# Mixer A's heads in two passes, branch products in pieces beside them, and the out product made once

## The chip, the cores and the metric

The kernel runs on one core of one Trainium2 chip. The metric is the device time of one execution in microseconds (us). TensorE (PE) does the matmuls, VectorE (DVE), ScalarE (ACT) and GpSimd (POOL) work elementwise, and SyncE (SP) issues nearly all DMA transfers. Each engine runs its own instruction list strictly in the order in which it was written, and waits at semaphores for the others.

## The reference, cut to what matters

One layer of an encoder with two parallel mixers, over 1024 prompt tokens and 32 new tokens of another stream, which the kernel lays side by side as 1056 columns:

```python
h = rmsnorm(x) @ w_in          # -> q/k/v and indexer of mixer A, q/k/v of mixer B, gates ga, gb
o_a = sparse_attention(...)    # mixer A, 8 heads of 64: top-k mask, softmax
o_b = stick_breaking(...)      # mixer B, 8 heads of 64: sigmoid products from the right
m = sigmoid(ga) * (o_a @ w_branch_a) + sigmoid(gb) * (o_b @ w_branch_b)
h = x + m @ w_out              # 1024 x 1024
y = h + relu(rmsnorm(h) @ w_up)**2 @ w_down      # 1024 -> 4096 -> 1024
```

All of it is float32.

## The kernel before

**Three matmuls for one product.** Every float32 operand is split into a high part `h` (a cast to `fp32r` on ACT) and a low part `l = x - h` (on POOL or DVE). A product is three matmuls: `wh xh + wh xl + wl xh` (`three`). A weight unit is a 128x512 tile: its DMA to `wst`, its cast on ACT (`wh`) and its subtraction on POOL (`wl`); five such units can be held at a time (`WB`).

**Column blocks.** `column_block` makes one 128-row block of a product over all tokens, in the chunks `self.parts`: columns 0-511, 512-783 and 784-1055 (widths 512, 272, 272). Columns 0-511 are "tile 0" of a pair of tiles, columns 512-1055 "tile 1" (`pick`).

**Attention.** `attend(h, is_a)` makes one head. It has two halves: `i = 0` for query tiles t = 0 to 3 (128 tokens each) and `i = 1` for t = 4 to 7. For each query tile there are scores against all earlier keys (PE, tile `s`), for mixer A a masked maximum on DVE, an exponential on ACT, a reciprocal on DVE and a normalisation on POOL (tile `p`). For each pair of query tiles follow transposes (PE, `t<-ident,p`), a split of the transposed weights into two parts (ACT cast and DVE subtraction, tile `tt`), the product with the values (PE, `o<-tt,v`), and `halves`, which adds the two parts (ACT copy and DVE addition, tile `o`) before the output goes to DRAM (`do`). Keys, values and queries are loaded from DRAM for each head. `attend_new` does the 32 new tokens of four heads at once.

**Work beside the heads.** The gate products (16 blocks `gate(e)`, 8 of each mixer) and the branch products of mixer B (8 blocks `branch_b(e)`, all three chunks at once) are put between the heads by `GATES_BESIDE` and `BRANCH_BESIDE`. A `with nc.behind()` makes each DMA recorded in it wait for the last instruction recorded before it, that is for the store of the head before.

**The order.** The kernel records its operations in a list and places them itself (`Plan`): an operation runs when what it needs is there, by rank (`FAST`, `PREP`, `MAIN`, `FILL`), and the matmuls of column blocks have the rank `FILL`, behind those of attention. So the order on each engine is fixed when the program is built, by a table of assumed costs. All operations are recorded at one line of the kernel, L387, so the profile's rows are told apart by tile names.

**After the heads.** `merge` loads mixer A's head outputs (`load_o`, tile `oa`), makes the branch product of mixer A (tile `ft` takes gate times product, POOL adds mixer B's part `y`, and ACT and DVE split the sum into `mh` and `ml`), and then the out product: for tokens 0-511 all eight blocks `e` in chunks of 256, then for tokens 512-1055 all eight in chunks of 272, so that each of the 16 units of `w_out` is loaded and split twice. After each block from the fifth on, `h_forms` cuts the result (tile `y`) into high and low parts of sums and differences that the FFN needs as operands: seven forms, `B11`, `B21` in `xl`, `T1`, `B22` in `oa`, `T2`, `T3` in `mh` and `T4` in `ml`. Those in `mh` and `ml` overwrite the out product's own operands.

**The FFN** (`ffn`, `down`) takes the seven forms in the order B11, B21, T1, T2, T3, T4, B22, 24 matmuls of 256 or 272 columns each, per pair of row blocks.

Of the kernel before, what the change touches and what calls it, by code (L numbers as in the profile page):

```python
# [27 lines left out]
H = 8  # L28
# [16 lines left out]
GATES_BESIDE = (1, 1, 1, 1, 1, 1, 1, 0, 1, 0, 0, 0, 0, 0, 0, 0)  # L45
BRANCH_BESIDE = (0, 0, 0, 0, 2, 2, 2, 2)
# [348 lines left out]

class Layer:
# [82 lines left out]
    def run(self):  # L479
# [113 lines left out]
        todo = iter(range(KB))  # L593
        for h in range(H):
            self.attend(h, True)
            if h in (2, 5):
                self.attend_new(h // 3, True)
            with nc.behind():
                for _ in range(GATES_BESIDE[H + h]):
                    self.gate(next(gates), "gz", 3)  # L600
                if h == 3:
                    self.yy = [nc.tile(xp, [128, KB, n], F32, f"y{i}", tag=f"xh{i}") for i, n in enumerate((W1, T - W1))]
                    ob = self.xl
                    self.load_o(ob, 4, range(4))
                for _ in range(BRANCH_BESIDE[h]):
                    self.branch_b(next(todo), ob)
# [486 lines left out]
    def attend(self, h, is_a):  # L1093
# [33 lines left out]
        for i in range(2):  # L1127
# [28 lines left out]
    def attend_new(self, u, is_a):  # L1156
# [92 lines left out]
    def branch(self, name, e, o, done):  # L1249
# [3 lines left out]
            [unit], lambda k, cs: (self.pick(o, k, cs), self.pick(o, 4 + k, cs)), done, self.parts, kn=4)  # L1253

    def branch_b(self, e, o):

        nc = self.nc
        with nc.rank(PREP):
            nc.sync.dma_start(self.yy[0][:, e], self.dg[KB + e, :, 0:W1])
# [6 lines left out]
        self.branch("w_bb", e, o, done)  # L1266
# [15 lines left out]
    def merge(self):  # L1282

        nc, a, f32 = self.nc, self.a, lambda z: z.bitcast(F32)
        self.load_o(self.oa, 0, range(4))
        high = lambda k, cs: self.pick(self.mh, k, cs)
        low = lambda k, cs: self.pick([z[k // 4] for z in self.ml], k % 4, cs)
        sgs = self.ring(self.temps(self.ft, 4, 0, 544))
        for e in range(KB):

            def done(c, cs, ps, e=e):
# [5 lines left out]
                h, l = high(e, cs), low(e, cs)  # L1297
                nc.scalar.copy(h, sg)
                nc.vector.tensor_sub(l, sg, f32(h))

            self.branch("w_ba", e, self.oa, done)
# [10 lines left out]
        slots = self.ring(self.temps(self.ft, 9, 0, 272))  # L1312
        acc = self.rb
        for i in range(2):
            n, lo = QUADS[i]
            chunks = [slice(lo, lo + n), slice(lo + n, lo + 2 * n)]
            for e in (0, 4, 1, 5, 2, 6, 3, 7):
                units = [self.unit(a["w_out"][e, j]) for j in range(2)]

                def done(c, cs, ps, e=e, n=n):  # L1320
                    hs = slots()[:, :n]
                    with nc.rank(PREP):
                        nc.sync.dma_start(hs, a["xT"][:, e, cs])
                    nc.vector.tensor_add(hs, ps, hs)
                    nc.sync.dma_start(self.dh[e, :, cs], hs)
                    nc.scalar.activation(self.pick(self.yy, e, cs), hs, AF.Copy, scale=self.gf[:, e:e + 1])
                    if e == 0:
                        nc.scalar.activation(acc[:, cs], hs, AF.Square)
                    else:
# [16 lines left out]
    def cut(self, i, f, k, x):  # L1346
# [4 lines left out]
        nc.gpsimd.tensor_sub(l, x, h.bitcast(F32))  # L1351
# [336 lines left out]
```

## Time and profile before

| | |
|---|---|
| times of three runs | 1751.46, 1755.16, 2347.33 us; median 1755.16 us |
| profiled execution | 1752.31 us, span 1750.2 us |
| PE, PEld busy | 1705.4 us (97%), 1619.5 us (93%), 12584 matmuls |
| DVE, ACT, POOL busy | 1294.6 (74%), 948.7 (54%), 1000.7 us (57%) |
| HBM | 187.29 MB read, 86.78 MB written, 157 GB/s over the span |
| mean granted TensorE clock | 0.998 |

The span is the time from the first to the last instruction on the core. A matmul's shown duration overlaps the next one's: what one costs is the distance between two starts. Stages in the span: mixer B's heads from about 500 us, mixer A's from about 700 to 907 us, the branch product of A from 923 to 975 us, the out product to 1078 us, the FFN to the end.

### The profile page before, as it was taken

Reading aid. Unit: us, or ns where it says so; the run is one execution under the profiler, and the core shown is the slowest. Engines: PE = TensorE matmul, PEld = TensorE weight load, DVE = VectorE, ACT = ScalarE, POOL = GpSimd, SP = SyncE. Lnnn points to the kernel's source line nnn. Section 1 sums busy time; section 2 is a strip of 40 time slices with the busy share of each in tenths; the row PEclk is TensorE's granted clock in tenths of the full one; section 3 lists DMA queues with packets and bytes.
Section 4 is the critical chain, followed back from the end, with each engine's and each line's share of the span. In section 5 each row is a group of like instructions: output and inputs, shape, how many; then the busy total and the mean of one; then the engine's idle time right before and its main releaser. Section 6 shows DMA issues by size and latency. Waiting matters only on the chain. (4 is left out here: it accounts for less than half of the span.)

```text
span 1750.2 us, 35569 instructions
## 1 busy us (share of the span) xinstructions
PE 1705.4 (97%) x12584; PEld 1619.5 (93%) x12584; DVE 1294.6 (74%) x2678; ACT 948.7 (54%) x1997; POOL 1000.7 (57%) x863
## 2 busy tenths in 40 slices
PE   7999999999999999998899999999999999999998
PEld 7988898999989998897798998999999999999998
DVE  8577899999477988776654546876666696787667
ACT  7356888732367777898743565333333354335431
POOL 5822331344277676344638899876667775464442
PEclk9999999999999999999999999999999999999999
DMA  7233553444574555545654564344444486657644
GB/s 253 73 98 109 147 158 102 123 148 128 158 201 114 155 137 158 138 125 150 175 164 148 175 188 118 129 149 142 140 150 141 143 313 226 218 166 240 225 143 149
DMA packets 182338, 276.52 MB, mean 158 GB/s; under 512 B 30353, under 2 KB 71921, under 8 KB 182161
## 3 DMA queue, kind: packets, MB, share of 16 engines
q1 hardware_dynamic: 181728, 273.91, 51.0%
q8 instruction: 99, 1.62, 0.4%
q14 instruction: 79, 0.64, 0.1%
q10 hardware_dynamic: 432, 0.34, 0.1%
HBM read 187.29 MB, written 86.78 MB: 157 GB/s over the span
## 5 line engine op out<-in xcount | busy, mean ns | idle before, releaser
L387 POOL TENSOR_TENSOR wl<-wst,wh 128x512 fp32r<-128x512 f32 x197 | 274.0, 1400 | 222.4 <-ACT wh L387 204.9
L387 PE MATMUL pj<-xl,wh 128*128 128x272 f32 (+2 forms) x1232 | 349.9, 318 | 1.6 <-DVE ft L387 1.2
L387 PE MATMUL pj<-xh,wh 128*128 128x272 f32 (+1 forms) x768 | 251.6, 328 | 2.6 <-ACT wh L387 1.6
L387 PE MATMUL pj<-xh,wl 128*128 128x272 f32 (+1 forms) x768 | 252.0, 329 | 0.4 <-POOL wl L387 0.4
L387 PEld LDWEIGHTS pj<-xl,wh 128*128 128x128 f32 x1232 | 219.4, 188 | 15.5 <-DVE ft L387 1.5
L387 ACT CAST wh<-wst 128x512 fp32r<-128x512 f32 x197 | 120.9, 620 | 128.0 <-PE pj L387 25.1
L387 POOL TENSOR_TENSOR wl<-us,wh 128x512 fp32r<-128x512 f32 x80 | 119.7, 1502 | 115.9 <-ACT wh L387 114.3
L387 PEld LDWEIGHTS pj<-xh,wh 128*128 128x128 f32 x768 | 144.7, 188 | 13.5 <-ACT wh L387 1.8
L387 PEld LDWEIGHTS pj<-xh,wl 128*128 128x128 f32 x768 | 144.5, 188 | 11.5 <-POOL wl L387 0.6
L387 POOL TENSOR_TENSOR wl<-y,wh 128x512 fp32r<-128x512 f32 x79 | 109.2, 1387 | 39.6 <-ACT wh L387 37.9
L387 ACT CAST wh<-us 128x512 fp32r<-128x512 f32 x80 | 49.6, 621 | 142.6 <-DVE us L387 38.3
L387 DVE TENSOR_TENSOR_SCAN rem<-rem 128x384 f32<-128x384 f32 (+8 forms) x66 | 114.8, 1761 | 14.8 <-ACT rem L387 12.4
L387 POOL TENSOR_TENSOR p<-p,rem 128x383 f32<-128x383 f32 (+8 forms) x66 | 102.1, 1566 | 40.3 <-DVE rem L387 20.8
L387 DVE TENSOR_TENSOR tt<-t,tt 128x512 fp32r<-128x512 f32 (+2 forms) x168 | 99.7, 619 | 16.8 <-ACT tt L387 16.1
L387 PE MATMUL o<-tt,v 128*128 128x256 f32 (+1 forms) x640 | 100.4, 284 | 11.0 <-ACT tt L387 5.3
L387 PEld LDWEIGHTS o<-tt,v 128*128 128x128 f32 x640 | 90.9, 192 | 19.9 <-ACT tt L387 7.0
L387 PE MATMUL s<-k,q 128*128 128x512 f32 (+3 forms) x384 | 100.8, 358 | 3.3 <-DVE mx L387 1.3
L387 ACT ACTIVATE junk<-score,cand 128x1024 bf16<-128x1024 f32 (+2 forms) x93 | 96.9, 1042 | 12.3 <-DVE cand L387 11.0
L387 PE MATMUL s<-wh,xh 128*128 128x256 f32 (+1 forms) x360 | 101.0, 286 | 2.5 <-DVE small L387 1.9
L387 PE MATMUL s<-wh,xl 128*128 128x256 f32 (+1 forms) x360 | 100.9, 283 | 0.0
L387 PE MATMUL s<-wl,xh 128*128 128x256 f32 (+1 forms) x360 | 100.6, 282 | 0.0
L387 ACT CAST tt<-t 128x512 fp32r<-128x512 f32 (+2 forms) x168 | 84.9, 540 | 26.6 <-PE o L387 13.2
(326 smaller groups left out, 5592.6 us busy)
## 6 DMA issues: line engine op xcount, KB each, us to landing
us<-w_down SPq DMA_DIRECT2D x96, 256.0 KB, 2.9
q<-dq SPq DMA_DIRECT2D x64, 256.0 KB, 4.2
du<-y SPq DMA_DIRECT2D x56, 264.0 KB, 2.1
du<-us SPq DMA_DIRECT2D x56, 264.0 KB, 2.3
y<-w_up SPq DMA_DIRECT2D x44, 256.0 KB, 2.7
xl<-du SPq DMA_DIRECT2D x35, 264.0 KB, 5.4
mh<-du SPq DMA_DIRECT2D x35, 264.0 KB, 5.3
dv<-vs SPq DMA_DIRECT2D x32, 256.0 KB, 2.6
```

The source lines that it names most:

```text
L387: fn(*args, **kw)
```

## The change

- `attend` takes `passes`. Mixer A's heads run in two passes: first all eight heads with `passes=(0,)` (query tiles 0 to 3), then all eight with `(1,)` (query tiles 4 to 7, for which the first half of keys and values is loaded again).
- Five gate blocks instead of seven lie beside mixer B's heads, and three instead of one beside A's.
- The branch products are cut into pieces of one token part: `branch_b0(e)` (B, columns 0-511, gated, stored back to `dg` in DRAM), `branch_b1(e)` (B, the other two chunks, into `y`), `branch_a0(e)` (A, columns 0-511, added to `y` on POOL). A list of 27 pieces (3 gates, 8 + 8 + 8) is handed out beside the 16 half heads by `FILL_BESIDE`, each weight unit being loaded once per piece.
- `merge` makes only chunks 1 and 2 of A's branch product, and splits columns 0-511 of `y` that are there already.
- The out product runs once over all tokens: eight blocks `e` with chunks 512, 272, 272. The square of the result is put back into PSUM by ACT, and DVE, not POOL, adds it up. `h_forms` runs for both token parts after each block from the fifth on, and the cuts for T2 (subtraction now on DVE), T3 and T4 follow for both parts at the end.

```diff
-GATES_BESIDE = (1, 1, 1, 1, 1, 1, 1, 0, 1, 0, 0, 0, 0, 0, 0, 0)
-BRANCH_BESIDE = (0, 0, 0, 0, 2, 2, 2, 2)
+GATES_BESIDE = (1, 1, 1, 1, 1, 0, 0, 0)
+FILL_BESIDE = (1, 1, 1, 1, 2, 2, 2, 2, 2, 2, 2, 2, 2, 2, 2, 2)
...
+        fill = [(lambda e: self.gate(e, "gz", 3), e) for e in gates]
+        fill += [(self.branch_b0, e) for e in range(KB)]
+        fill += [(self.branch_b1, e) for e in range(KB)]
+        fill += [(self.branch_a0, e) for e in range(KB)]
+        fill = iter(fill)
...
         for h in range(H):
-            self.attend(h, True)
+            self.attend(h, True, (0,))
+            beside(FILL_BESIDE[h])
+        for h in range(H):
+            self.attend(h, True, (1,))
             if h in (2, 5):
                 self.attend_new(h // 3, True)
...
+            beside(FILL_BESIDE[H + h] if h < H - 1 else None)
+        self.load_o(self.xl, 0, range(1, 2))
...
+    def branch_a0(self, e):
...
+        y = self.yy[0][:, e]
+        with nc.rank(PREP):
+            nc.sync.dma_start(y, self.dg[KB + e, :, 0:W1])
+        self.gated("w_ba", e, self.dg[e], lambda z: nc.gpsimd.tensor_add(y, y, z))
...
-        for i in range(2):
-            n, lo = QUADS[i]
-            chunks = [slice(lo, lo + n), slice(lo + n, lo + 2 * n)]
-            for e in (0, 4, 1, 5, 2, 6, 3, 7):
...
+        for e in (0, 4, 1, 5, 2, 6, 3, 7):
+            units = [self.unit(a["w_out"][e, j]) for j in range(2)]
...
-                        sq = slots()[:, :n]
-                        nc.scalar.activation(sq, hs, AF.Square)
-                        nc.gpsimd.tensor_add(acc[:, cs], acc[:, cs], sq)
+                    nc.scalar.activation(ps, hs, AF.Square)
+                    nc.vector.tensor_add(acc[:, cs], ps, acc[:, cs])
...
+        for f, eng in ((T2, nc.vector), (T3, nc.gpsimd), (T4, nc.gpsimd)):
+            for i in range(2):
                 for k in range(4):
-                    self.cut(i, f, k, self.h_parts(i, k)[{T2: 3, T3: 0, T4: 2}[f]])
+                    self.cut(i, f, k, self.h_parts(i, k)[{T2: 3, T3: 0, T4: 2}[f]], eng)
```

**First place: PE where mixer A begins.** Rows of PE shortly after mixer B's last head (`s`, `t`, `o` are attention; `pj` is a gate block with its weights `wh`, `wl`). Before:

```order
L387 MATMUL pj<-xl_108,wh_6828 128x272
L387 MATMUL pj<-xh_107,wl_6829 128x272
L387 MATMUL pj<-xh_105,wh_6916 128x512
L387 MATMUL pj<-xl_106,wh_6916 128x512
L387 MATMUL pj<-xh_105,wl_6917 128x512
L387 MATMUL o<-tt,v 128x256
L387 MATMUL pj<-xh_105,wh_6916 128x512
L387 MATMUL pj<-xl_106,wh_6916 128x512
L387 MATMUL pj<-xh_105,wl_6917 128x512
L387 MATMUL pj<-xh_105,wh_6916 128x512
L387 MATMUL o<-tt,v 128x256 x4
```

After the change, behind the same two rows of the last gate block (`wh_6828`, `wl_6829`):

```order
L387 MATMUL pj<-xl_108,wh_6828 128x272
L387 MATMUL pj<-xh_107,wl_6829 128x272
L387 MATMUL o<-tt,v 128x256 x5
L387 MATMUL t<-ident,p 128x128 x3
L387 MATMUL o<-tt,v 128x256 x3
L387 MATMUL t<-ident,p 128x128 x4
L387 MATMUL s<-k,q 128x256 x2
L387 MATMUL s<-k,q 128x384 x2
L387 MATMUL o<-tt,v 128x256
L387 MATMUL s<-k,q 128x512 x2
L387 MATMUL s<-k,q 128x128 x2
L387 MATMUL o<-tt,v 128x256
```

The next gate block has moved back: behind these two rows come 42 rows of half heads without a `pj` matmul, and then the first of the three gates.

**Second place: POOL at the end of mixer A, after the change.** `wl..<-wst` is a weight unit's low part, `y0<-y0,gz` the addition of one `branch_a0` piece, `xl1` the low part of A's head outputs, `ft<-ft,y1` an addition in `merge`:

```order
L387 TENSOR_TENSOR y0_7311<-y0_7311,gz_7718 128x512
L387 TENSOR_TENSOR wl4_7774<-wst_7772,wh4_7773 128x512
L387 TENSOR_TENSOR y0_7311<-y0_7311,gz_7723 128x512
L387 TENSOR_TENSOR wl2_7766<-wst_7764,wh2_7765 128x512
L387 TENSOR_TENSOR xl1_108<-xl1_108 128x544
L387 TENSOR_TENSOR y0_7311<-y0_7311,gz_7768 128x512
L387 TENSOR_TENSOR wl0_12717<-wst_12715,wh0_12716 128x512
```

The low part of the last `branch_a0` unit (`wl2_7766`, e = 7) stands behind the addition of the piece e = 6 (`gz_7723`), where before whole blocks of mixer B's branch product were the last work beside the heads.

**Third place: POOL where the FFN begins.** Before (`rb` is the sum of squares; `oa`, `xl`, `mh`, `ml` are cuts):

```order
L387 TENSOR_TENSOR xl1_108<-y1_7342,xl1_108 128x272
L387 TENSOR_TENSOR wl0_12419<-wst_12403,wh0_12418 128x512
L387 TENSOR_TENSOR wl1_12423<-wst_12405,wh1_12422 128x512
L387 TENSOR_TENSOR rb_109<-rb_109,ft_12230 128x272
L387 TENSOR_TENSOR oa1_12223<-y1_7342,oa1_12223 128x272 x2
L387 TENSOR_TENSOR xl1_108<-y1_7342,xl1_108 128x272 x2
```

After the change:

```order
L387 TENSOR_TENSOR xl1_108<-y1_7312,xl1_108 128x272
L387 TENSOR_TENSOR ml00_12706<-y0_7311,ml00_12706 128x256 x2
L387 TENSOR_TENSOR oa1_12703<-y1_7312,oa1_12703 128x272
L387 TENSOR_TENSOR mh0_12704<-y0_7311,mh0_12704 128x256 x3
L387 TENSOR_TENSOR ml00_12706<-y0_7311,ml00_12706 128x256
L387 TENSOR_TENSOR ml10_12708<-y1_7312,ml10_12708 128x272
L387 TENSOR_TENSOR xl0_106<-y0_7311,xl0_106 128x256
L387 TENSOR_TENSOR oa0_12702<-y0_7311,oa0_12702 128x256
L387 TENSOR_TENSOR mh1_12705<-y1_7312,mh1_12705 128x272
L387 TENSOR_TENSOR xl1_108<-y1_7312,xl1_108 128x272
L387 TENSOR_TENSOR mh1_12705<-y1_7312,mh1_12705 128x272
L387 TENSOR_TENSOR wl4_12831<-y0_7311,wh4_12830 128x512
```

Before, the cuts for `xl1` and `oa1` of most of the blocks still stand behind the last addition to `rb`, and those of `mh0` and `ml00` are past; after, the cuts of `mh0` and `ml00` stand among the last block's.

More of the change, by code (lines that the diff above doesn't have):

```diff
@@ L1125, in weights @@
             return self.stick_weights(parts, L, *room)
-        for i in range(2):
+        for i in passes:
             o = nc.tile(at, [64, 512], F32, "o", bufs=2)
@@ L1235, in pick, with load_o @@
         return tiles[i][:, k, cs.start - i * W1:cs.stop - i * W1]
-    def load_o(self, o, g, es):
+    def load_o(self, o, g, groups):
         nc = self.nc
-        for e in es:
-            for i, (lo, hi) in enumerate(((0, W1), (W1, T))):
+        for e in range(4):
+            for i in groups:
+                lo, hi = ((0, W1), (W1, T))[i]
                 h, l = o[i][:, e], o[i][:, 4 + e]
@@ L1264, in done @@
             nc.vector.tensor_mul(y, ps, y)
-        self.branch("w_bb", e, o, done)
+        self.branch("w_bb", e, self.xl, done, self.parts[1:])
     def ring(self, views):
@@ L1288, in merge, with split @@
         sgs = self.ring(self.temps(self.ft, 4, 0, 544))
+        def split(e, cs, y):
+            nc.scalar.copy(high(e, cs), y)
+            nc.vector.tensor_sub(low(e, cs), y, f32(high(e, cs)))
+        for e in range(KB):
+            with nc.rank(PREP):
+                split(e, self.parts[0], self.yy[0][:, e])
         for e in range(KB):
@@ L1296, in done @@
                 nc.gpsimd.tensor_add(sg, sg, self.pick(self.yy, e, cs))
[L1297 to L1301, printed above, removed]
+                split(e, cs, sg)
+            self.branch("w_ba", e, self.xl, done, self.parts[1:])
         self.forms = []
@@ L1311, in merge @@
             self.forms.append(f)
-        slots = self.ring(self.temps(self.ft, 9, 0, 272))
+        slots = self.ring(self.temps(self.ft, 4, 0, 544))
         acc = self.rb
-        for i in range(2):
-            n, lo = QUADS[i]
-            chunks = [slice(lo, lo + n), slice(lo + n, lo + 2 * n)]
-            for e in (0, 4, 1, 5, 2, 6, 3, 7):
[L1318 to L1329, printed above, removed]
-                        sq = slots()[:, :n]
-                        nc.scalar.activation(sq, hs, AF.Square)
-                        nc.gpsimd.tensor_add(acc[:, cs], acc[:, cs], sq)
-                self.column_block(units, lambda k, cs: (high(k, cs), low(k, cs)), done, chunks)
-                if e >= 4:
@@ new lines, in merge, with done @@
+        for e in (0, 4, 1, 5, 2, 6, 3, 7):
+            units = [self.unit(a["w_out"][e, j]) for j in range(2)]
+            def done(c, cs, ps, e=e):
+                hs = slots()[:, :cs.stop - cs.start]
+                with nc.rank(PREP):
+                    nc.sync.dma_start(hs, a["xT"][:, e, cs])
+                nc.vector.tensor_add(hs, ps, hs)
+                nc.sync.dma_start(self.dh[e, :, cs], hs)
+                nc.scalar.activation(self.pick(self.yy, e, cs), hs, AF.Copy, scale=self.gf[:, e:e + 1])
+                if e == 0:
+                    nc.scalar.activation(acc[:, cs], hs, AF.Square)
+                else:
+                    nc.scalar.activation(ps, hs, AF.Square)
+                    nc.vector.tensor_add(acc[:, cs], ps, acc[:, cs])
+            self.column_block(units, lambda k, cs: (high(k, cs), low(k, cs)), done, self.parts)
+            if e >= 4:
+                for i in range(2):
```

76 lines of the change are left out of this document (49 added, 27 removed).

## The prediction

> **What bounds the kernel now.** First the page's busy times, then a table of stages, then PE's instructions one by one.
>
> ```profile
> PE 1705.4 (97%) x12584; PEld 1619.5 (93%) x12584; DVE 1294.6 (74%) x2678; ACT 948.7 (54%) x1997; POOL 1000.7 (57%) x863
> ```
>
> PE is busy nearly all the time, so an edit counts only if it removes PE's work or PE's waits. Where the waits lie is in the table of busy times by stage (span, then for PE, PEld, DVE, ACT, POOL the busy time and the number of instructions, the granted clock, the DMA share and GB/s):
>
> ```profile
> 700.00:798.00 98.00, 96.09 (x678) 89.12 (x677) 71.13 (x240) 91.63 (x165) 39.91 (x46) 1.00 0.51 137
> 798.00:848.00 50.00, 40.39 (x255) 33.62 (x253) 33.59 (x110) 41.22 (x85) 28.15 (x30) 0.93 0.55 160
> 848.00:975.00 127.00, 125.81 (x825) 114.66 (x825) 75.52 (x188) 58.06 (x122) 71.63 (x68) 1.00 0.51 155
> 975.00:1078.00 103.00, 103.00 (x849) 103.00 (x848) 48.78 (x73) 62.46 (x151) 96.65 (x100) 1.00 0.64 185
> 1078.00:1112.00 34.00, 28.56 (x187) 24.31 (x186) 31.04 (x46) 13.10 (x31) 32.54 (x33) 1.00 0.13 40
> 1150.00:1350.00 200.00, 200.00 (x1645) 200.00 (x1644) 134.19 (x253) 73.54 (x164) 144.39 (x108) 1.00 0.43 142
> ```
>
> Two stages of these wait: 798 to 848 us (mixer A's heads with no gate or branch block beside them) and 1078 to 1112 us (the start of the FFN). Busy time understates a wait, since each matmul's shown end covers part of the gap behind it; so I count matmuls instead. The dense FFN row gives 200 / 1645 = 0.1216 us per matmul of 256 or 272 columns. The other prices come from distances between starts:
>
> ```profile
> 709.45 2.02 PE L387 MATMUL o<-tt,v 128*128 128x256 f32 x16
> 711.30 1.06 PE L387 MATMUL t<-ident,p 128*128 128x128 f32 x8
> 712.12 0.72 PE L387 MATMUL s<-k,q 128*128 128x512 f32 x2
> 712.68 0.29 PE L387 MATMUL pj<-xh,wh 128*128 128x272 f32 x1
> 712.80 0.29 PE L387 MATMUL pj<-xl,wh 128*128 128x272 f32 x1
> 712.92 0.29 PE L387 MATMUL pj<-xh,wl 128*128 128x272 f32 x1
> 713.05 0.39 PE L387 MATMUL pj<-xh,wh 128*128 128x512 f32 x1
> 713.28 0.39 PE L387 MATMUL pj<-xl,wh 128*128 128x512 f32 x1
> ```
>
> A value product costs (711.30 - 709.45) / 16 = 0.116 us, a transpose 0.82 / 8 = 0.103, a 272-column matmul (713.05 - 712.68) / 3 = 0.123, a 512-column one 0.23. The groups of PE from 798 to 848 us, costliest first:
>
> ```profile
> L387 PE MATMUL o<-tt,v 128*128 128x256 f32 x77 | 15.5, 319 | 7.3 <-DVE o L387 3.9 <-ACT tt L387 3.1 <-DVE tt L387 0.3
> L387 PE MATMUL t<-ident,p 128*128 128x128 f32 x87 | 14.5, 299 | 0.0
> L387 PE MATMUL s<-k,q 128*128 128x512 f32 x20 | 6.9, 427 | 0.8 <-DMA q<-dq 0.5 <-DVE mx L387 0.2
> ```
>
> These make 77 x 0.116 + 87 x 0.103 + 20 x 0.23 = 22.5 us; the other 71 matmuls, at an estimated 0.13 each, 9.2. So PE had 31.6 us of work in 50 us: **18.4 us of waiting**. At the FFN's start 187 x 0.1216 = 22.7 us of work stand in 34 us: **11.3 us of waiting**. The out product (975 to 1078 us) has PE at 103.00 of 103 us, so there only its own work can shrink.
>
> **The change part by part.**
>
> *Heads and pieces.* The work beside the heads no longer ends before the last heads, so the 18.4 us go: the order has pieces between the half heads of the whole second pass. There I expect what the covered rows show, 98 - 96.09 = 1.9 us idle in 98 and 1.2 us in 127, as before. What is late next is the first pass. The order's 42 rows of half heads without a `pj` matmul show that its gates are not there in time: each piece's weights may be loaded only after the store of a half head. A half head is 8 score matmuls (two each of 512, 384, 256, 128 columns; 384 estimated at 0.175), 10 transposes and 12 value products: 1.25 + 1.03 + 1.39 = 3.67 us of PE. DVE's prices, from its groups between 700 and 920 us:
>
> ```profile
> L387 DVE TENSOR_TENSOR tt<-t,tt 128x512 fp32r<-128x512 f32 x55 | 37.0, 683 | 4.3 <-ACT tt L387 4.1
> L387 DVE CUSTOM_DVE_ANT_0 p<-s,mask 128x512 f32<-128x512 f32 x42 | 28.2, 683 | 4.6 <-PE t L387 3.6 <-PE s L387 0.9
> L387 DVE TENSOR_TENSOR tt<-t,tt 128x384 fp32r<-128x384 f32 x36 | 19.5, 548 | 7.0 <-ACT tt L387 6.8
> L387 DVE TENSOR_TENSOR o<-o 64x256 f32<-64x256 f32 x38 | 15.7, 413 | 13.9 <-ACT o L387 13.2 <-DMA v<-dv 0.7
> L387 DVE TENSOR_SCALAR nb<-mx,fq 128x1 f32<-128x1 f32 x64 | 12.7, 204 | 1.8 <-POOL p L387 0.4
> L387 DVE RECIPROCAL nb<-nb 128x1 f32<-128x1 f32 x66 | 9.9, 156 | 15.2 <-ACT p L387 14.5
> ...
> L387 DVE CUSTOM_DVE_ANT_0 p<-s,mask 128x384 f32<-128x384 f32 x7 | 3.9, 555 | 4.7 <-PE t L387 4.7
> ...
> L387 DVE CUSTOM_DVE_ANT_0 p<-s,mask 128x256 f32<-128x256 f32 x8 | 3.3, 418 | 0.0
> ...
> L387 DVE CUSTOM_DVE_ANT_0 p<-s,mask 128x128 f32<-128x128 f32 x8 | 2.3, 283 | 2.3 <-PE t L387 2.3
> ```
>
> A half head of the first pass takes 0.683 + 0.555 + 0.418 + 0.283 for the four maxima, 4 x (0.204 + 0.156) for the one-column steps, 0.683 + 2 x 0.548 for the splits and 2 x 0.413 for the halves: 6.0 us of DVE against 3.67 of PE. Eight half heads are 48 us of DVE against 29.4 of PE; with some 50 gate matmuls that the order has in this stretch (7 us) PE has 36. If DVE never waits, PE waits 12 us. The nearest row on how full an elementwise engine gets is 700 to 798 us, ACT at 91.63 of 98 (93%): DVE at 93% gives 48 / 0.93 - 36 = 15.6. I take **14 us**. Upper end: the share of waiting in the uncovered stretch, 18.4 / 31.6 of 36, 21 us. Lower end: six `p` buffers let DVE do maxima 1.5 half heads ahead (2.8 us each), 8 us.
>
> *The end of the heads.* Before, whole branch blocks covered it. Now the unit of the last `branch_a0` piece may be loaded only after the last head's store.
>
> ```profile
> q<-dq SPq DMA_DIRECT2D x64, 256.0 KB, 4.2
> ```
>
> Behind the last value product come the two steps of `halves` (0.4 each), store and load (at most 4.2 each, the dearest landing among head loads), cast (0.6) and POOL (1.4, with one addition of 1.3 queued ahead by the order): 12.5 us. PE's cover by the order is three and a third pieces of 12 x 0.23, 9.2 us. A wait of 3.3 by this dear price; I take **2.5 us**, ends 0 and 5. A matmul waiting for that low part holds back all of A's remaining branch product, for PE runs in order.
>
> *More transfers.* Keys and values of the first half are loaded twice (8 x 512 KB), the gated piece is stored and loaded back (16 x 256 KB), and weights come about 16 times more beside the heads (4.2 MB): some 13 MB in 200 us, 65 GB/s on top of 137. The DMA share would go from 0.51 to about 0.75. SP issues them in the slots where it waited. I price this at 0; if the cover goes, it shows as PE waiting for `q<-dq`, 0.5 us now.
>
> *Merge and out product.* POOL's prices from 975 to 1112 us:
>
> ```profile
> L387 POOL TENSOR_TENSOR wl<-wst,wh 128x512 fp32r<-128x512 f32 x33 | 44.8, 1372 | 3.3 <-ACT wh L387 3.2
> L387 POOL TENSOR_TENSOR rb<-rb,ft 128x272 f32<-128x272 f32 x14 | 12.4, 883 | 1.0 <-ACT ft L387 0.7 <-DMA wst<-w_up 0.2
> ...
> L387 POOL TENSOR_TENSOR oa<-y,oa 128x272 fp32r<-128x272 f32 x8 | 6.6, 844 | 0.0
> ```
>
> A's remaining branch block is 24 x 0.123 = 2.95 us of PE and, on POOL, 1.372 + 2 x 0.883 = 3.14: eight blocks wait about **1 us** (0 to 10, see rivals). The out product's 768 matmuls, 192 x 2 x (0.120 + 0.123) = 93.3 us, become 576: 192 x (0.23 + 2 x 0.123) = 91.4; I take **-1 us**. Sixteen units fewer (16 x 1.372 = 22 us) and the sums of squares (28 x 0.8 = 23 us) leave POOL, which was at 96.65 of 103 us; that pays only at the FFN's start.
>
> *The FFN's start.* From the third place in the order to the last cut of T4, POOL has 22 cuts and 6 units: 22 x 0.85 + 6 x 1.4 = 27 us. It can begin when the last block's first chunk is done, 48 x 0.123 = 5.9 us before the out product's end, so it ends 22 us behind that end. PE asks for the second token part of T4 after five products of 24 x 0.1216 = 2.92 us and half of one, at 16 us. **6 us** of waiting instead of 11.3. Ends: 2, if later products fill in as the order lets some do, and 11, as before.
>
> Sum against the profiled execution's 1752.3 us: -18.4 + 14 + 2.5 + 1 - 1 - 5.3 = -7.2, so **1745 us**. The median of the runs, 1755.16, is 2.9 us above that execution; a change of 2% (to 1720 or 1790) is about the least that a measurement of this kernel can tell from none.
>
> **Rivals.**
>
> *A, the waits close.* First pass 8, end 0, FFN 2: -18.4 + 8 + 0 + 1 - 1 - 9.3 = -19.7, 1733 us. For it: PE did not wait from 700 to 798 us although ACT was at 93%. Against it: DVE's 6.0 us per half head against 3.67.
>
> *B, slower: the first pass at half clock.* The trace has one such case:
>
> ```profile
> 802.01 0.29 PE L387 MATMUL o<-tt,vn 32*128 32x64 f32 x1
> 804.96 1.43 PE L387 MATMUL o<-tt,v 128*128 128x256 f32 x5 [2.66 <-DVE o L387]
> ```
>
> ```profile
> 803.90:810.70 6.80, 5.74 (x26) 5.39 (x27) 4.66 (x12) 4.95 (x14) 1.52 (x3) 0.50 0.68 227
> ```
>
> One idle time of 2.66 us was followed by a granted clock of 0.50 for 6.8 us. If the half heads of the first pass each leave PE idle that long in one piece, every 6.8 us or so, its 36 us of work run at half clock: 36 us of waiting for the 14, 1767 us. Against it: 18.4 us of waiting held only one such gap; DVE's and PE's work interleave in pieces under 2 us. The Trainium skill, "TensorE: Matmul & The Clock Gate", section "What's actually happening", says that the clock falls to half after an idle window of about 3.4 us whose phase is free-running; the 6.8 us here are two such windows, while the idle time was shorter than one. By that page gaps under 3.4 us would cost no clock, which would take this rival's ground away; the trace shows that 2.66 can be enough.
>
> *C, POOL at the end of the heads.* From the first `branch_a0` piece on, POOL has 8 x (1.3 + 1.37) + 8 x 3.14 = 46 us against PE's 8 x (2.76 + 2.95) = 46, with the last normalisations and `xl1` on top. If it enters 10 us behind, PE waits those: 1755 us.
>
> That the pieces do not come beside the heads is excluded by the order.
>
> **How the numbers follow.** Forecast (1737 to 1753) 0.55, A 0.22, B 0.10, C 0.13. The range goes from 1728, 5 us under A's sum because the covered stretches' 3 us of idle and half of the remaining FFN wait could go too, to 1764, which leaves out most of B. A time under 1720 needs every wait gone, 0.03; over 1790, B with the other stretches too, 0.03.
>
> **What would show it.** Right: 1733-1764 us with no idle stretch in the second pass, the count of PE's matmuls falling short in the first 50 us of mixer A by about 14 us, a single wait for `wl` or `xl` where the heads end, and the FFN's start with 5 to 7 us for POOL's `mh` and `ml`. Wrong: a granted clock under 1.00 in the first pass (B), PE waiting for `ft` or `wl` through A's branch product (C), or PE waiting for `q<-dq`.

## The result, and the profile after

| | before | after |
|---|---|---|
| median of four runs each | 1755.24 us | 1739.78 us (1736.45 to 1741.50) |
| ratio of times | | 0.9917, interval 0.9892 to 0.9941 |
| profiled execution, span | 1752.31, 1750.2 us | 1739.05, 1737.1 us |

The kernel became 15.5 us faster by the medians, 13.3 us by the two profiled executions. That is under 2%, but the interval of the ratio, a quarter of a per cent to each side, leaves out 1, so less than the prediction's 2% can be told from none here. The forecast was 1745 us, with 1728 to 1764 as its range: direction and range were right, and the gain was about twice the 7.2 us of the sum. (Among the runs of before, one of 2347.33 us was disturbed and is left out of the ratio.)

The page's busy times of the changed kernel:

```profile
PE 1701.1 (98%) x12392; PEld 1611.0 (93%) x12392; DVE 1291.6 (74%) x2699; ACT 941.1 (54%) x1977; POOL 971.5 (56%) x827
```

PE has 4.3 us less busy time, with 192 matmuls fewer, as the out product's 768 became 576. What else was won is waiting time, so the stages are read next. The table of busy times by stage, changed kernel (span, then busy time and instructions of PE, PEld, DVE, ACT and POOL, granted clock, DMA share, GB/s):

```profile
702.00:745.00 43.00, 38.43 (x254) 32.61 (x253) 35.57 (x155) 40.86 (x101) 18.98 (x31) 1.00 0.82 220
710.00:735.00 25.00, 21.12 (x137) 16.97 (x135) 23.05 (x100) 24.65 (x61) 10.92 (x20) 1.00 0.80 222
745.00:798.00 53.00, 53.00 (x367) 48.81 (x366) 33.54 (x100) 47.34 (x80) 22.93 (x24) 1.00 0.53 165
798.00:848.00 50.00, 49.63 (x297) 43.20 (x296) 29.87 (x90) 37.56 (x71) 35.57 (x33) 1.00 0.90 273
928.00:950.00 22.00, 19.30 (x101) 16.35 (x100) 8.82 (x12) 9.06 (x16) 17.16 (x14) 0.92 0.54 161
967.00:1068.00 101.00, 101.00 (x648) 92.55 (x647) 56.69 (x101) 55.28 (x132) 65.14 (x68) 1.00 0.49 149
1058.00:1110.00 52.00, 48.34 (x358) 45.98 (x357) 51.88 (x73) 21.23 (x50) 41.52 (x33) 0.97 0.30 97
```

Four places answer to the prediction.

**The uncovered heads are gone.** From 798 to 848 us PE shows 49.63 of 50 us busy where it had 40.39, with 297 instead of 255 matmuls. By the prediction's prices (0.13 for the small shapes) the 297 are about 48.8 us of work, so some 17 of the 18.4 us of waiting went.

**The first pass waits, mostly in one place.** Its last half head ends shortly before 745 us; from there on, in the second pass, PE is full. PE falls short above all from 710 to 735 us. The groups of PE in these 25 us, changed kernel:

```profile
L387 PE MATMUL t<-ident,p 128*128 128x128 f32 x47 | 7.0, 276 | 0.2 <-DVE tt L387 0.2
L387 PE MATMUL o<-tt,v 128*128 128x256 f32 x34 | 6.7, 307 | 1.2 <-DVE o L387 0.5 <-DVE tt L387 0.3 <-ACT tt L387 0.2
L387 PE MATMUL s<-k,q 128*128 128x512 f32 x8 | 2.7, 414 | 0.2 <-DVE mx L387 0.2
L387 PE MATMUL s<-k,q 128*128 128x384 f32 x8 | 2.5, 388 | 0.8 <-DVE mx L387 0.7
L387 PE MATMUL s<-k,q 128*128 128x256 f32 x10 | 2.4, 323 | 1.3 <-DVE mx L387 1.3
L387 PE MATMUL o<-tt,v 128*128 128x128 f32 x14 | 2.4, 249 | 0.0
L387 PE MATMUL s<-k,q 128*128 128x128 f32 x9 | 1.9, 262 | 0.0
```

With the prediction's prices per matmul these are 47 x 0.103 + 34 x 0.116 + 8 x 0.23 + 8 x 0.175 + 10 x 0.122 + (14 + 9) x 0.103 (the last taken as the transposes' price) = 15.6 us. The other 7 of the 137 matmuls are `pj`, the products put beside the heads: 4 of 272 and 3 of 512 columns, 1.2 us. So 16.8 us of work stand in 25 us: **8.2 us of waiting**, and only 7 covering matmuls in the whole stretch. The same count gives 9.8 us for the whole of 702 to 745 us, and for the kernel before 2.6 and 2.9 us.

**The end of the heads.** PE one by one, then POOL one by one, changed kernel:

```profile
939.13 0.50 PE L387 MATMUL pj<-og,wl 128*128 128x512 f32 x1 [2.70 <-POOL wl L387]
```

```profile
936.59 1.26 POOL L387 TENSOR_TENSOR y<-y,gz 128x512 f32<-128x512 f32 x1 [0.27 <-DVE gz L387]
937.81 1.26 POOL L387 TENSOR_TENSOR wl<-wst,wh 128x512 fp32r<-128x512 f32 x1
```

This is the single wait that was forecast, at its size (2.5 predicted, 2.70 measured), with the one addition of 1.26 us queued ahead of `wl` on POOL. What was not forecast comes behind it. The granted clock (column before the DMA share) in two stretches right after a wait:

```profile
940.30:943.70 3.40, 3.40 (x13) 2.84 (x12) 0.69 (x1) 1.29 (x3) 0.18 (x2) 0.51 0.75 232
1100.80:1104.20 3.40, 3.09 (x14) 2.79 (x13) 3.40 (x7) 0.65 (x2) 0.00 (x0) 0.50 0.28 77
```

3.4 us at half clock cost 1.7 us more, so the end of the heads costs 2.7 + 1.7 = 4.4 us.

**The FFN's start.** In the 52 us from shortly before its first matmul PE has 358 matmuls. At 0.1216 us each that is 43.5 us of work: 8.5 us of waiting. The same stretch of the kernel before, with 336 matmuls, had 40.9 us of work and 11.1 us of waiting:

```profile
1068.00:1120.00 52.00, 46.56 (x336) 42.31 (x335) 45.13 (x66) 20.69 (x49) 49.80 (x48) 1.00 0.25 78
```

Between the two rows the engine that is full changes: POOL 49.80 of 52 us before, DVE 51.88 of 52 after. PE's waits at this place, changed kernel (engine, what it makes, what it waited for: total, times, longest):

```profile
PE pj L387 <- DVE ft L387: 2.1, 2, 1.7
PE c L387 <- DVE ft L387: 0.8, 1, 0.8
PE b L387 <- DVE ft L387: 0.5, 2, 0.3
PE pj L387 <- POOL mh L387: 0.3, 1, 0.3
```

and the wait that the second of the half-clock stretches above follows:

```profile
1099.55 0.51 PE L387 MATMUL pj<-xl,wh 128*128 128x256 f32 x2 [1.75 <-DVE ft L387]
```

The named releaser is `ft` on DVE, an eviction of a PSUM bank, and not POOL's cuts.

### The profile page after: what moved, and what is told of

It reads as the page before. It is cut to its first block, busy times and chain, and to the rows that moved or that the text cites. A ratio compares the mean times of both kernels' runs of the same rounds, so it can differ in the third digit from the quotient of the medians.

```text
span 1737.1 us, 35119 instructions
## 1 busy us (share of the span) xinstructions
PE 1701.1 (98%) x12392; PEld 1611.0 (93%) x12392; DVE 1291.6 (74%) x2699; ACT 941.1 (54%) x1977; POOL 971.5 (56%) x827
## 4 chain that ended last, share of the span: by engine, by line
PE 83%; DVE 9%; DMA 3%; issue 3%; ACT 1%; POOL 1%; SPq 0%; ACTq 0%; DVEq 0%; POOLq 0%
PE pj L387 32%; PE s L387 11%; PE a L387 11%; PE c L387 10%; PE b L387 10%; PE t L387 5%; PE o L387 4%; DVE junk L387 2%; DVE y L387 1%; DMA xt<-x 1%; ACT p L387 1%; POOL wl L387 1%; DVE ft L387 0%; DVE pre L387 0%; DMA q<-dq 0%
## 5 line engine op out<-in xcount | busy, mean ns | idle before, releaser
L387 PE MATMUL pj<-xl,wh 128*128 128x272 f32 (+2 forms) x1200 | 336.8, 313 | 1.7 <-DVE ft L387 1.7
L387 PEld LDWEIGHTS pj<-xl,wh 128*128 128x128 f32 x1200 | 213.8, 189 | 13.3 <-DVE ft L387 2.0
L387 PEld LDWEIGHTS pj<-xh,wh 128*128 128x128 f32 x768 | 144.7, 188 | 14.2 <-ACT wh L387 2.2
L387 ACT CAST wh<-y 128x512 fp32r<-128x512 f32 x79 | 49.1, 622 | 100.4 <-issue 19.9
```

The source lines that it names most:

```text
L387: fn(*args, **kw)
```

## The experiments

Three theories stood: (1) the first pass waits because its cover is thin, and cover alone decides; (2) the end of the heads waits because the last piece's weights queue behind the last store; (3) the FFN's start waits for DVE. Their rivals were the half heads themselves, ScalarE as the bound of the first pass, and POOL's cuts. The times, each against the kernel before on the same chip:

| run | median us | ratio to before | interval |
|---|---|---|---|
| changed kernel | 1739.78 | 0.9917 | 0.9892 to 0.9941 |
| e1_heads_only | 1751.31 | 0.9984 | 0.9970 to 0.9997 |
| e2_out_only | 1749.01 | 0.9977 | 0.9968 to 0.9987 |
| e3_one_pass | 1749.84 | 0.9975 | 0.9960 to 0.9990 |
| e4_tail | 1734.99 | 0.9897 | 0.9880 to 0.9913 |
| e5_norm_spread | 1735.92 | 0.9889 | 0.9874 to 0.9903 |
| e6_tanh | 1741.56 | 0.9924 | 0.9909 to 0.9939 |
| e7_gates7 | 1745.05 | 0.9940 | 0.9918 to 0.9961 |
| e8_cover | 1738.65 | 0.9899 | 0.9879 to 0.9919 |
| e9_cover_norm | 1737.45 | 0.9893 | 0.9872 to 0.9914 |
| e10_cover_norm_tanh | 1731.52 | 0.9864 | 0.9849 to 0.9879 |
| e11_tail_norm | 1731.47 | 0.9866 | 0.9850 to 0.9883 |

### The two parts alone: e1_heads_only, e2_out_only

The first is the changed kernel with the old out product, the second the old heads with the new one; the part that is exchanged is the loop:

```diff
-        for e in (0, 4, 1, 5, 2, 6, 3, 7):              # new: once, self.parts
+        for i in range(2):                              # old: once per token part
+            for e in (0, 4, 1, 5, 2, 6, 3, 7):
...
-        for f, eng in ((T2, nc.vector), (T3, nc.gpsimd), (T4, nc.gpsimd)):
+            for f in (T2, T3, T4):
```

> The changed kernel with the out product of the kernel before (two token parts, squares added on POOL); heads in two passes and pieces stay. Theory 1 (the gain is cover for mixer A's heads): against the kernel before the time falls by 8 to 10 us, to about 1743-1747; PE waits some 9 us in the first pass and 5 us where the heads end, and the 11 to 12 us of waiting at the FFN's start stay. Rival (the out product and the FFN's start carry the gain): it falls by 4 us at most.

> The kernel before with the new out product alone (once over all tokens, squares on DVE, T2's subtractions on DVE). Theory 1: the time falls by about 3 us, to 1752; the 19 us of waiting in mixer A's uncovered heads stay, and the FFN's start waits 8 to 9 us instead of 11.6. Rival: it falls by 9 us or more.

Measured: 2.5 and 4.8 us under before by the medians, together 7 of the 15.5, so the parts help each other. The time of e1 is the rival's (4 us at most), but its waits are the theory's: by the count of matmuls 10.3 us in the first pass, 4.6 us from 928 to 950 us, and 1.5 us from 798 to 848 us. What it won in the heads it lost behind them, first at the FFN's start. The same 52 us there, heads alone and then out product alone:

```profile
1061.00:1113.00 52.00, 46.33 (x307) 41.77 (x306) 44.49 (x58) 19.84 (x47) 50.76 (x51) 0.90 0.25 79
```

```profile
1071.00:1123.00 52.00, 48.36 (x358) 45.89 (x357) 51.88 (x73) 21.64 (x51) 41.88 (x33) 0.97 0.31 98
```

307 matmuls are 37.3 us of work, 14.7 of waiting, against 11.1 before; 358 leave 8.5, as in the changed kernel. With the old out product POOL is the full engine again (50.76 of 52), and PE waits for it in small pieces. In the heads-only run these were followed by 10.2 us at half clock, a length that only e7 has once more. Wait row and clock row of e1:

```profile
PE b L387 <- POOL oa L387: 1.9, 3, 1.2
```

```profile
1079.30:1089.50 10.20, 9.00 (x34) 7.56 (x34) 10.13 (x12) 4.80 (x12) 10.20 (x11) 0.50 0.11 27
```

So in these profiled runs the new out product is worth 11.1 - 8.5 = 2.6 us at this place with the old heads and 14.7 - 8.5 = 6.2 us with the new. The heads alone lost 3.6 us here, and the half-clock stretch, worth up to 5.1 us, is enough to account for it. The rest fits the clock as well: away from the program's ends the profiled run of e1 has 27.2 us at half clock (at 297.5, 720.8, 942.6, 1079.3 and 1550.2 us), before has 6.8 and the changed kernel 10.2. Its ten runs point the same way: the three from 1745.97 to 1748.98 us have a mean granted clock of 0.996 to 0.997, the four from 1752.87 to 1754.12 us 0.991 to 0.995. Why the heads alone fall to half clock more often is not shown.

### Whole heads with the cover spread: e3_one_pass

```diff
-GATES_BESIDE = (1, 1, 1, 1, 1, 1, 1, 0, 1, 0, 0, 0, 0, 0, 0, 0)
-BRANCH_BESIDE = (0, 0, 0, 0, 2, 2, 2, 2)
+GATES_BESIDE = (1, 1, 1, 1, 1, 0, 0, 0, 1, 1, 1, 0, 0, 0, 0, 0)
+BRANCH_BESIDE = (0, 0, 0, 1, 2, 2, 2, 1)
```

> The kernel before with its two tables changed alone: five gate blocks beside mixer B, three beside mixer A's first three heads, and the whole branch blocks of mixer B as 1, 2, 2, 2, 1 beside A's heads 3 to 7; heads in one pass, no pieces. Theory 1 (only cover counts): PE's waits in mixer A fall from 19 us to about 6 and the time to about 1742, as with two passes. Rival (two passes are needed, since ScalarE is full and whole blocks of B do not last to the end): at least 13 us of waits stay, and the time is 1749 or more.

This is the kernel before, with nothing but its two tables changed: two gates move from B's heads to A's, and the branch blocks of B start one head earlier. Measured 1749.84 us: the theory (1742) missed, and the rival's figure (1749 or more, 13 us of waits or more) held. By stage:

```profile
710.00:735.00 25.00, 19.80 (x137) 17.11 (x136) 19.50 (x68) 22.61 (x47) 9.73 (x13) 1.00 0.35 90
798.00:848.00 50.00, 49.55 (x357) 46.32 (x357) 34.32 (x108) 45.46 (x85) 29.16 (x28) 1.00 0.59 181
1063.00:1115.00 52.00, 46.43 (x318) 42.35 (x317) 43.85 (x60) 19.96 (x47) 50.49 (x48) 0.93 0.24 74
```

The second row shows that tables alone cover the stretch from 798 to 848 us (49.55 of 50). The first shows the early wait of the changed kernel with whole heads, 7.9 us by the count: the half heads do not make it. But the waits only moved: over all of mixer A's heads, 702 to 928 us, the count gives 22.7 us of waiting, against 28.5 before and 16.5 in the changed kernel. So cover does not do the whole by tables alone; whether the rest needs half heads or only smaller pieces was not tested. The third row has 318 matmuls, 38.7 us of work and 13.3 of waiting, 2.2 more than before, with a clock of 0.93 where before had 1.00: part of the gain is lost here too.

### The last piece handed out one head earlier: e4_tail

```diff
-FILL_BESIDE = (1, 1, 1, 1, 2, 2, 2, 2, 2, 2, 2, 2, 2, 2, 2, 2)
+FILL_BESIDE = (1, 1, 1, 1, 2, 2, 2, 2, 2, 2, 2, 2, 2, 2, 3, 3)
```

> The changed kernel with the last branch_a0 piece handed out one half head earlier (third last entry of FILL_BESIDE 3 instead of 2), so that its weights wait for the store of head 6 and not of head 7. Theory 2 (the wait of 2.7 us for a low part where the heads end is the hold of those weights): the gap and the half-clock spell of 3.4 us behind it go, 4.4 us less than the changed kernel, 1735. Rival (the head's own output, stored and loaded back, comes as late): PE waits for xl instead, and at most 1 us is won.

The entry that acts is the second last, behind head 6; behind head 7 comes what is left. Measured 1734.99 us, 0.9897. The end of the heads in this run:

```profile
928.00:950.00 22.00, 22.00 (x136) 19.89 (x135) 13.20 (x16) 10.98 (x21) 20.50 (x17) 1.00 0.52 155
```

136 matmuls instead of 101, and the full clock: the wait for `wl` and the half-clock stretch behind it are both gone. By ratio the gain on the changed kernel is 0.0020 of 1755, 3.5 us, beside the 4.4 of the profile.

### norm in four pieces: e5_norm_spread

`norm`, which turns the FFN's sums of squares into factors, is four pieces of five DVE instructions each (a reciprocal and what goes around it), all recorded behind the FFN's first pair of row blocks, `p == 0`. The edit puts one piece each behind the pairs 2, 4, 6 and 8:

```diff
-        def norm():
-            for i, (n, lo) in enumerate(QUADS):
-                for c in range(2):
+        def norm(part):
+            for i, (n, lo) in [(part // 2, QUADS[part // 2])]:
+                for c in (part % 2,):
...
-            if p == 0:
-                norm()
+            if p in (2, 4, 6, 8):
+                norm(p // 2 - 1)
```

> The changed kernel with one edit: the per-half work of norm (sums, reciprocals, products) is made in four pieces spread through its branch product instead of all in front. Theory (VectorE's norm at the FFN's start holds the evictions that TensorE waits for, 41.9 of 42 us busy there): TensorE's waits between 1068 and 1110 us fall from some 8.9 us to 2-4, the half-clock stretch behind them goes, and the time falls by 4 to 6 us, to about 1734-1736. Rival (GpSimd's cuts at the end of the out product set this wait): at most 1 us.

Measured 1735.92 us. First the two groups of `norm`'s reciprocals, among DVE's dearest at the FFN's start of the changed kernel, then the stage in e5:

```profile
L387 DVE RECIPROCAL rb<-ft 128x272 f32<-128x272 f32 x2 | 3.7, 1839 | 0.0
L387 DVE RECIPROCAL rb<-ft 128x256 f32<-128x256 f32 x2 | 3.5, 1739 | 0.0
```

```profile
1059.00:1111.00 52.00, 51.73 (x415) 50.78 (x415) 46.63 (x75) 25.16 (x60) 44.78 (x36) 1.00 0.40 128
```

415 matmuls are 50.5 us of work: the waiting falls from 8.5 to 1.5 us. The edit leaves POOL's cuts as they were. So the FFN's start waited for DVE's `norm`, and the rival (POOL) is out. Of the 7.0 us the ratio shows 0.0028 of 1755, 4.9 us: some of it comes back where the pieces lie now, and the end of the heads had a longer half-clock stretch in the profiled run. From 1110 to 1200 us the changed kernel has 741 matmuls and e5 724, 17 x 0.1216 = 2.1 us fewer. The half-clock stretch of e5 at the end of the heads:

```profile
938.40:945.20 6.80, 5.91 (x17) 4.94 (x18) 0.69 (x1) 1.62 (x4) 2.54 (x3) 0.50 0.40 127
```

### ScalarE relieved: e6_tanh

```diff
-            nc.scalar.activation(z, z, AF.Sigmoid)
+            nc.scalar.activation(z, z, AF.Tanh, scale=0.5)
+            nc.gpsimd.tensor_scalar(z, z, 0.5, 0.5, op0=ALU.mult, op1=ALU.add)
```

> The changed kernel with the gates' sigmoid made as 0.5*tanh(x/2)+0.5, the 0.5s on GpSimd, so that ScalarE changes its table 6 times instead of 23 in the program. Theory (ScalarE, 95% busy between 702 and 745 us with five table loads of 1283 ns, is the bound of mixer A's first pass): TensorE's waits there fall from some 9 us to 3-5, the time by 4 to 6 us. Rival (the cover beside the half heads is too thin, or VectorE sets the pace): at most 1 us.

Measured 1741.56 us: no gain (0.9924 against 0.9917). The table loads of the changed kernel and of e6, then the stage in e6:

```profile
L387 ACT ACT_TABLE_LOAD x23 | 29.5, 1283 | 2.6 <-issue 2.3
```

```profile
L387 ACT ACT_TABLE_LOAD x6 | 7.7, 1283 | 3.3 <-issue 2.3 <-DMA wst<-w_g 0.9
```

```profile
702.00:745.00 43.00, 36.17 (x254) 31.63 (x253) 38.66 (x146) 35.87 (x92) 22.99 (x31) 1.00 0.77 204
```

ACT falls from 40.86 to 35.87 us in these 43, and PE is busy for 36.17 us instead of 38.43, with 254 matmuls in both. So the theory that ScalarE's table loads bound the first pass found no support. The test is not quite clean, since the covering matmuls from 710 to 735 us fell from 7 to 0 as well; but five half heads took 23.56 us there (711.68 to 735.24 us) with ACT at 20.64 and DVE at 20.70 us, against 24.05 us in the changed kernel with ACT at 23.67. The pace hardly changed although no engine was full.

### Seven gates beside B again: e7_gates7

```diff
-GATES_BESIDE = (1, 1, 1, 1, 1, 0, 0, 0)
-FILL_BESIDE = (1, 1, 1, 1, 2, 2, 2, 2, 2, 2, 2, 2, 2, 2, 2, 2)
+GATES_BESIDE = (1, 1, 1, 1, 1, 1, 1, 0)
+FILL_BESIDE = (1, 1, 1, 1, 1, 1, 2, 2, 2, 2, 2, 2, 2, 2, 2, 2)
```

> The changed kernel with the two gate units that it moved out of mixer B's heads back beside them (seven gates beside B's heads, none at the start of A's), the branch pieces as before. Theory (the two gates bring ScalarE's evictions and table loads into A's first pass, and that is where its waits come from): waits between 702 and 745 us fall from 9 us to 2-4, the time by about 5 us, less what B's heads lose. Rival (the first pass waits because its units are half heads): the waits stay at 8 us or more, the time within 1 us.

Measured 1745.05 us, slower than the changed kernel. Two stages of e7:

```profile
702.00:745.00 43.00, 42.86 (x302) 39.67 (x301) 30.57 (x113) 40.86 (x82) 14.28 (x22) 1.00 0.78 218
893.00:915.00 22.00, 18.41 (x77) 14.54 (x76) 13.23 (x48) 9.54 (x19) 11.50 (x13) 0.78 0.46 133
```

The early wait is gone, with the same half heads and with ACT at the very same 40.86 us of 43. But the cover now runs out late: from 893 to 915 us there are 77 matmuls in 22 us, and the clock falls to 0.78. Only five of them are `pj` matmuls, and from 848 to 928 us the count gives 15.0 us of waiting in e7, against 2.4 in the changed kernel. The cover is one budget: what lies at the seam is missing at the end. The same count at the seam, 710 to 735 us, for four kernels (before, changed, e6, e7: `pj` matmuls with their busy time, clock, DMA share, GB/s):

```profile
710.00:735.00 25.00, 12.04 (x52) 1.00 0.44 124
```

```profile
710.00:735.00 25.00, 1.56 (x7) 1.00 0.80 222
```

```profile
710.00:735.00 25.00, 0.00 (x0) 1.00 0.72 183
```

```profile
710.00:735.00 25.00, 14.30 (x66) 1.00 0.74 199
```

Before and e7, with 52 and 66, wait little (2.6 and 0.5 us by the count); the changed kernel and e6, with 7 and 0, wait 8.2 and 7.9.

### A gate at the seam: e8_cover, e9_cover_norm, e10_cover_norm_tanh

```diff
-GATES_BESIDE = (1, 1, 1, 1, 1, 0, 0, 0)
+GATES_BESIDE = (1, 1, 1, 0, 1, 1, 0, 1)
```

e9 adds the edit of e5; e10 adds that of e6 as well, with a table of its own, (1, 1, 1, 1, 1, 1, 0, 1).

> The changed kernel with one table changed: GATES_BESIDE (1,1,1,0,1,1,0,1) instead of (1,1,1,1,1,0,0,0), so that the last gates beside mixer B's heads start later and one more of them lies at the seam to mixer A's; in TensorE's order no stretch of more than 5 us of head work is left without a pj product between its pieces (the changed kernel has one of 12 us, where the waits at 710-735 us are), and one piece fewer is left behind the last head. Theory (the waits lie where the order has no cover, whatever engine is named as the one waited for): waits from the seam to the end of the heads fall from some 18 us to 6-8, the time to 1729-1733. Rival (the cover is one budget, and what is filled at the seam is missing at another place): the waits move to other heads, the time stays within 3 us of 1739.8.

> The table of the run before and norm in four pieces together. Theory (two separate causes): the FFN's start waits 2 us instead of 9 and the heads as in the run before, 1724-1729. Rival (what is won at one place is given back at another): no lower than the better of the two by itself.

> The run before with the sigmoid by tanh (6 table loads instead of 23) and GATES_BESIDE (1,1,1,1,1,1,0,1), with which TensorE's order again has no bare stretch over 5 us. Theory (with the order covered, ScalarE's table loads lie beside TensorE's work): within 3 us of the run before. Rival (the 17 loads of 1283 ns still hold evictions for TensorE): 4 to 8 us below it.

Measured 1738.65, 1737.45 and 1731.52 us. For e8 this is a miss: the time stayed within 3 us of 1739.8, as its rival said. The `pj` matmuls at the seam are 37 (e8):

```profile
710.00:735.00 25.00, 10.14 (x37) 0.93 0.80 211
```

PE still waited there, once for 1.86 us, and 3.4 us at half clock followed; and the wait at the end of the heads came at another unit and was longer. The two half-clock stretches of e8; the second one began in a wait of 3.62 us for `wl` that ended at 949.15 us:

```profile
722.70:726.10 3.40, 3.40 (x15) 3.21 (x14) 2.15 (x9) 3.35 (x10) 2.96 (x4) 0.50 1.05 216
947.90:954.70 6.80, 5.55 (x24) 5.55 (x25) 6.53 (x9) 1.07 (x3) 5.55 (x5) 0.50 0.58 160
```

So an order without a bare stretch over 5 us is not enough; more cover than 37 matmuls in 25 us, or shorter gaps, is needed for no waiting, and moving a gate forward thinned the end. e9 keeps both of these waits, and its gain on e8 (1.2 us) is inside the intervals; it missed its 1724 to 1729 us, and its rival (no lower than the better of the two alone, e5's 1735.92) held. e10 is 6 us below e9, which its rival (the table loads) expected, but its own table gave it more cover at both places: at the seam 58 `pj` matmuls and, from 702 to 745 us, 2.4 us of waiting against e9's 7.3, and from 928 to 950 us 137 matmuls at clock 1.00 against e9's 115 at 0.95. Whether fewer table loads helped at all in e10 cannot be told, since its table differs.

### The two edits that worked: e11_tail_norm

The edits of e4 and e5 on the changed kernel, the gates as the change had them.

> The changed kernel with the two single edits that gave most: the last branch piece of mixer A handed out after head 6 (FILL_BESIDE ending in 2, 3, 3) and norm in four pieces; its gates stay where the change put them. Theory (these two waits are independent of each other: some 4.8 us at the end of the heads and 7 us at the FFN's start, of which the norm edit alone gave back about 3 elsewhere): 1729-1732. Rival (a wait taken away only lets the next one come, so that the gains do not add): 1734-1736, as each of the two alone.

Measured 1731.47 us (1729.80 to 1732.45): the gains add. By ratio e4 gave 0.0020 and e5 0.0028 on the changed kernel, and e11 0.0051. The intervals of e4 and e5 still overlap that of the changed kernel, and that of e11 (0.9850 to 0.9883) does not; so the times bear out the two edits together, and for each alone it is the trace that shows the wait gone. The FFN's start of e11:

```profile
1054.00:1106.00 52.00, 51.75 (x416) 50.81 (x415) 46.35 (x74) 25.00 (x59) 44.73 (x36) 1.00 0.40 125
```

1.4 us of waiting. With e10 it is the fastest version here, 23 us below before.

## Why the prediction was right, and where its sizes were off

| term | predicted us | by the profiles us |
|---|---|---|
| uncovered heads, 798 to 848 | -18.4 | about -17 |
| first pass | +14 | +9.8 where before had 2.9 |
| end of the heads | +2.5 | +2.7 and 1.7 for the clock |
| more transfers | 0 | 0 |
| A's remaining branch product | +1 | 0 |
| out product's own work | -1 | -1, not measured by itself |
| FFN's start | -5.3 | 8.5 - 11.1 = -2.6 |

The middle column adds to -7.2, the right one to about -9; the profiled executions differ by 13.3. The count of matmuls places most of the rest. The covered heads from 848 to 928 us wait 2.4 us instead of 4.7, mixer B's heads from 480 to 702 us 8.4 instead of 9.8; why is not shown. Against them stands a third half-clock stretch of the changed kernel, at 1537.6 us: the matmul just ahead of it starts 14.2 us earlier than in the kernel before (1536.79 against 1551.01), the end comes 13.1 earlier. One to two us stay unplaced. So the forecast owes its closeness to terms that were off in opposite directions.

**Uncovered heads: right.** Pieces lie beside the whole second pass, and PE is busy for 49.63 of 50 us.

**First pass: the mis-sized step.** The prediction found the place, the rows of half heads without a `pj` in the order, and forecast 14 us where the count gives 9.8. The term that failed is DVE's price of a half head. It is a sum of shown durations, 6.0 us, and DVE's durations overlap as PE's do. Two rows of DVE, then five half heads, from the first maximum over 384 columns of one to that of the fifth behind it, all of the changed kernel:

```profile
712.91 0.69 DVE L387 CUSTOM_DVE_ANT_0 p<-s,mask 128x512 f32<-128x512 f32 x1
713.52 0.21 DVE L387 TENSOR_SCALAR nb<-mx,fq 128x1 f32<-128x1 f32 x1
```

```profile
712.44:736.49 24.05, 20.48 (x133) 16.62 (x132) 21.52 (x95) 23.67 (x60) 12.11 (x21) 1.00 0.86 234
```

The maximum is shown with 0.69 us, and what comes behind it starts after 0.61. The five half heads took 24.05 us and 21.52 us of DVE, 4.3 each and not 6.0. Eight are 34 us, less than PE's 36, and at 93% the prediction's own argument would have given 34.4 / 0.93 - 36 = 1 us of waiting. So DVE's pace was not the cause that it was taken for, and that a wait of this order came is in part luck. Nor is the wait a price of half heads, for e3 has it with whole ones; e7 takes it away by moving two gates back to B's heads, so it comes with moving them out. And it does not follow the load of one engine. ACT at 40.86 of 43 us goes with waits in the changed kernel and without them in e7. DVE from 710 to 735 us is at 23.05 us in the changed kernel and 19.50 in e3, both with about 8 us of waiting, and at 20.07 in e7 with 0.5. As these rows read, PE in a bare stretch follows the chain from scores through DVE, ACT and POOL to the next product, and beside enough cover it does not; which link sets the 4.8 us per half head is not isolated.

**End of the heads: right in mechanism and size, with the clock left out.** The 12.5 us chain of halves, store, load, cast and POOL against 9.2 us of cover was worked out as a wait of 3.3 and taken as 2.5; it was 2.70. e4 confirms it by removing it.

**Transfers: right.** The DMA share rose more than the 0.75 that was worked out, to 0.90 from 798 to 848 us, and PE waited 0.6 us for `q<-dq` in the first pass and 0.4 us for `k<-dk` in all that followed it.

**A's remaining branch product: the ends of 0 to 10 held, at 0.** No wait of PE is listed between 944 and 967 us. Rival C is out.

**FFN's start: wrong in mechanism.** The prediction gave the 6 us to POOL's cuts of T3 and T4 (by its own sum 5, for 27 - 5.9 is 21 and not 22) and expected its `mh` and `ml` as releasers. PE waited 0.3 us for `mh`. POOL had only 65.14 of 101 us in the out product where it had 96.65 of 103, so it was no longer late; DVE was (51.88 of 52 us). Its `norm` stands in that very stretch in the kernel before too, but there POOL was the fuller engine (49.80 of 52 us, DVE 45.13), and PE waited most for it: 1.7 us for `oa` alone, against 1.5 us for `ft` on DVE. The question that the prediction asked elsewhere, what is late next, was answered here with the same engine again. e5 shows the cause.

**Rivals.** A (waits close, 1733 us) had the nearer first pass (8 us) but neither the end nor the FFN. B (half clock throughout the first pass) did not come; the clock was 1.00 there. But half-clock stretches did come behind single waits, and B's ground, that a wait of 2.66 us can do it, was right. The Trainium skill, "TensorE: Matmul & The Clock Gate", section "What's actually happening", puts the fall to half clock after a free-running window of about 3.4 us without work; every stretch shown here lasts 3.4 us or a multiple, which agrees, but they follow waits of 1.75, 1.86 and 2.70 us, shorter than that window.

## What to carry to other kernels

Price an instruction by the distance to the next start, on every engine and not only on PE. Count the covering products in the bounding engine's written order, stretch by stretch: a bare stretch costs waits whoever is named as the releaser, and cover moved to one place is missing at another, so price the bare stretch and not the whole pass. When an edit relieves the engine that was last at some place, list what the next engine has queued at that place before crediting the gain; here spreading `norm` on DVE, an edit of five lines, brought 4.9 us by the ratio, a third of what the whole change brought. Hand out the last piece of a sequence early enough that its weights do not queue behind the last store.

## What the runs showed of the hardware

- **A short wait can cost the clock.** Behind single PE waits of 1.67 us (1536.79 us, changed kernel), 1.75 us (1099.55 us, changed kernel), 1.86 us (e8) and 2.70 us (939.13 us, changed kernel) the granted clock was 0.50 or 0.51 for 3.4 us. The kernel before has the same 1.67 us at the same matmul (1551.01 us) and stays at full clock. A wait of the same 1.75 us in e6's first pass had none behind it:

```profile
726.88 0.59 PE L387 MATMUL s<-k,q 128*128 128x384 f32 x2 [1.75 <-DVE nb L387]
```

The length of the wait alone does not decide it. The traces show what goes with it. In each trace the half-clock stretches start whole multiples of about 3.41 us apart (in the changed kernel at 940.3, 1100.8 and 1537.6 us, 47 and 128 such steps). In the changed kernel PE was busy for half or less of the step just before each. These three steps, then the step of e6 that holds the larger part of its 1.75 us, whose beginning falls into the step before:

```profile
936.90:940.30 3.40, 1.17 (x5) 1.00 (x6) 0.00 (x0) 0.69 (x2) 3.40 (x3) 1.00 0.35 98
1097.40:1100.80 3.40, 1.65 (x14) 1.45 (x13) 3.40 (x5) 0.00 (x0) 2.88 (x2) 1.00 0.21 81
1534.20:1537.60 3.40, 1.68 (x12) 1.24 (x10) 3.40 (x8) 0.90 (x2) 0.78 (x1) 1.00 0.00 0
```

```profile
725.80:729.20 3.40, 2.32 (x18) 2.34 (x19) 2.01 (x13) 2.35 (x8) 1.52 (x3) 1.00 1.03 294
```

Over all thirteen traces, without the first 60 and the last 25 us, half clock followed 24 of the 25 such steps in which PE was busy for under 48%, 12 of the 46 between 48 and 65%, and 1 of some 6200 above. So it seems to matter how a wait falls into the steps, beside its length. This is read from the traces; no run was made to vary it.

- **A table load cost what its row says.** From 702 to 745 us ACT of the changed kernel has four of them and the end of a fifth, at 1283 ns:

```profile
L387 ACT ACT_TABLE_LOAD x5 | 6.4, 1283 | 0.1
```

The Trainium skill, "ScalarE: Activation LUTs", section "What ACT_TABLE_LOAD costs", adds about 1380 ns of drain to each switch. The trace does not show it as idle time: four drains would be 5.5 us, an estimate from that page, and leave ACT at most 37.5 of the 43 us, where it was busy for 40.86. Before and behind each load of the program but the first, ACT is idle for less than 0.02 us.
